# The scores' product with the keys' low parts takes all 128 rows of the query tile, in place of the 64 rows that hold its high parts

## The chip, the cores and the metric

The kernel runs on one core of one Trainium2 chip. The metric is the device time of one execution in microseconds (us). The program is static: each engine works through its own list of instructions in a fixed order, and waits on semaphores where it needs another engine's result.

## What is computed

The reference is a trunk of two layers. Each layer adds half a SwiGLU feed-forward, then a mixer of three head groups with one output projection, then half a second feed-forward. One of the three groups is sparse attention with 8 heads of width 64 in 2 groups. Its selected and its window branch both score every query against the keys of its past; here all 8 blocks of 64 keys are selected, so that both come out as causal attention over the 512 tokens:

```
s = einsum('bqgrd,bgqkd->bgrqk', qb, k_sel) * scale + bias_s      # selected branch
p = masked_softmax(s, d_s >= 0)
o_slc = einsum('bgrqk,bgqkd->bqgrd', p, v_sel)
s = einsum('bqgrd,bkgd->bgrqk', qb, kw) * scale + dense_bias(d_w) # window branch
p = masked_softmax(s, ok_w)
o_win = einsum('bgrqk,bkgd->bqgrd', p, vw)
```

## The kernel before

Nearly all products go through TensorE in a rounded 32-bit format (fp32r), and a 32-bit factor is split in two: a high part that the format holds, and a low part with the rest. A dense product then takes three matmuls in a row into the same PSUM bank (`mm3`, L224 to L226: high by high, high by low, low by high), each with a moving operand of 512 columns.

In the attention a head has only 64 rows of contraction. `nsa_q` (L1052) puts both parts of a query head in one tile of 128 rows: for the even head of a pair (e = 0) the high part is in rows 0 to 63 and the low part in rows 64 to 127, for the odd head (e = 1) the other way round. `nsa_k` (L1035) writes the keys' high part `kh` into both halves of a tile, and the keys' low part `kl` into both halves of another. The matmul at L1156 with `kh` over 128 rows therefore gives (q high + q low) by k high in one go. The matmul at L1159 adds q high by k low; for that it takes only the 64 rows with the high part, rows 0 to 63 for e = 0 and rows 64 to 127 for e = 1.

`scores` (L1143) does one unit: a pair of heads, one block of 128 queries (i = 0 to 3), and the two branches b. For each branch it takes two banks with the tag pS, which has two buffers, and writes four matmuls, of 256, 256, 384 or 512 columns for i = 0 to 3. VectorE then adds the bias and takes the row extreme (L1162), ScalarE exponentiates (L1166), TensorE transposes the weights (`turn`, L1182; its banks have the tags pS and pv by turns) and multiplies them with the values (`mix`, L1198; two heads go side by side, each on 64 columns of the array). There are 16 units in each of the two layers, so 128 matmuls at L1156 and 128 at L1159 in all.

The attention doesn't run alone. Generators for the dense projections, the recurrences, the attention and the output projection are merged by weights (`Weave`), and a scheduler then fixes each engine's order. So the four matmuls of a branch needn't stand together, and dense matmuls, transposes and value products stand between them. The names in the trace: psS is a bank of scores, q, kh and kl the tiles named above, ppt a bank of transposes, pno the attention's output bank, pd a bank of a dense product.

Of the kernel before, what the change touches and what calls it, by code (L numbers as in the profile page):

```python
# [62 lines left out]
class Trunk:  # L63
# [1061 lines left out]
    def nsa(self, st):  # L1125

        nc = self.nc
        v = nc.vector
        V, gates = st["v"], st["g"]
        T, pcT, po = {}, {}, {}  # L1130
        units = [(g, hp, i) for g in range(2) for hp in range(2) for i in range(4)]

        def start(g):
            while "k%d" % g not in st:
                yield 1.0
            T[g] = [self.bias_tile(4 * g + r) for r in range(4)]

        def cmp(g):
            while "vc" not in st:
                yield 1.0  # L1140
            pcT[g] = yield from self.nsa_cmp(g, T[g], st["k%d" % g][1], st["kc"], gates)

        def scores(g, hp, i):  # L1143

            h = 4 * g + 2 * hp
            KS, Q = st["k%d" % g]
            n = 128 * (i + 1)
            nm = max(n, 256)
            qs = slice(i * 128, (i + 1) * 128)
            mx, sm_ = self.s([128, 4], "mx"), self.s([128, 4], "smx")  # L1150
            P = [None] * 4
            for b in range(2):
                kh, kl = KS[b]
                ps = [self.pmt(name="psS", tag="pS") for _ in range(2)]
                for e in range(2):
                    nc.tensor.matmul(ps[e][:, :nm], Q[2 * hp + e][:, qs], kh[:, :nm], start=True, stop=False)  # L1156
                for e in range(2):
                    r = slice(64 * e, 64 * e + 64)
                    nc.tensor.matmul(ps[e][:, :nm], Q[2 * hp + e][r, qs], kl[r, :nm], start=False, stop=True)  # L1159
                for e in range(2):  # L1160
                    p = P[2 * e + b] = self.t2(name="P")
                    v.tensor_tensor_reduce(p[:, :n], T[g][2 * hp + e][:, L - n:], ps[e][:, :n], 1.0, 1e29, OP.add,  # L1162
                                           OP.min, mx[:, 2 * e + b:2 * e + b + 1])
                yield 0.25 + 0.15 * i
            for j in range(4):
                nc.scalar.activation(P[j][:, :n], P[j][:, :n], AF.Exp, bias=mx[:, j:j + 1], scale=-1.0,  # L1166
                                     accum_out=sm_[:, j:j + 1])
            v.tensor_scalar(sm_[:], sm_[:], TINY, None, op0=OP.max)
            v.reciprocal(sm_[:], sm_[:])
            v.tensor_tensor(sm_[:].rearrange("p (e b) -> p e b", e=2), sm_[:].rearrange("p (e b) -> p e b", e=2),  # L1170
                            gates[:, i, 3 * h:3 * h + 6].rearrange("p (e k) -> p e k", e=2)[:, :, 1:3], op=OP.mult)
            for j in range(4):
                v.tensor_scalar(P[j][:, :n], P[j][:, :n], sm_[:, j:j + 1], None, op0=OP.mult)
            return P

        def turn(i, P):
            R = []
            n = 128 * (i + 1)
            for k in range(4):
                pt = self.pmt(name="ppt", tag=("pS", "pv")[k % 2])  # L1180
                for j in range(i + 1):
                    nc.tensor.transpose(pt[:, j * 128:(j + 1) * 128], P[k][:, j * 128:(j + 1) * 128], self.idn[:])  # L1182
                PT = self.t2(name="PT")
                nc.scalar.copy(PT[:, :n], pt[:, :n])
                R.append(PT)
                if k % 2:
                    yield 0.2 * (i + 1)
            return R

        def mix(g, hp, i, R):  # L1190
            if i == 0:
                po[0] = self.pmt(name="pno", tag="po")
            qs = slice(i * 128, (i + 1) * 128)
            for b in range(2):
                for j in range(i + 1):
                    c = slice(g * 128 + 64 * b, g * 128 + 64 * b + 64)
                    for e in range(2):
                        nc.tensor.matmul(po[0][64 * e:64 * e + 64, qs], V[:, j, c], R[2 * e + b][:, j * 128:(j + 1) * 128],  # L1198
                                         start=i == 0 and b == 0, stop=False, skip_group_check=True)
            if i == 3:  # L1200
                nc.tensor.matmul(po[0][:], st["vc"][g][:, hp], pcT[g][:], start=False, stop=True, skip_group_check=True)  # L1201
                self.y[4 + 2 * g + hp] = self.split(po[0][:])
        P, R = {}, {}
        n = len(units)
        lt, lm = self.LAG
        yield from start(0)
        nxt = {}
        for g in range(2):
            nxt[8 * g + self.CMPU] = cmp(g)
        nxt[self.K1] = start(1)  # L1210
        run = []
        for k in range(n + lm):
            if k in nxt:
                run.append((k, nxt[k]))
            for j, q in list(run):
                for _ in range(1 if k < j + 2 else 10 ** 6):
                    try:
                        yield next(q)
                    except StopIteration:
                        run.remove((j, q))  # L1220
                        break
            if k < n:
                P[k] = yield from scores(*units[k])
            if 0 <= k - lt < n:
                R[k - lt] = yield from turn(units[k - lt][2], P.pop(k - lt))
            if 0 <= k - lm < n:
                mix(*units[k - lm], R.pop(k - lm))
                yield 0.44 * (units[k - lm][2] + 1)
# [269 lines left out]
```

## Time and profile before

| | |
|---|---|
| time, median of 3 runs (lowest to highest) | 2116.76 us (2115.8 to 2119.16) |
| the profiled execution: its time, its span | 2116.3 us, 2114.5 us |
| TensorE matmuls busy (share of the span) | 2091.4 us (99%) |
| TensorE weight loads busy | 1695.1 us (80%) |
| VectorE busy | 1188.1 us (56%) |
| ScalarE busy | 786.7 us (37%) |
| GpSimd busy | 82.8 us (4%) |

The span runs from the first to the last instruction in the trace; the profiled execution's time is 1.8 us above its span. An engine's busy time is the union of its instructions' durations. A matmul's duration overlaps the next one's, so what a matmul costs is read from start to start, or from the chain that ended last, which counts from end to end.

### The profile page before, as it was taken

How to read it: one execution, taken by the hardware profiler on the slowest of the kernel's cores; microseconds unless marked ns; L12 is line 12 of the kernel's file. 1: busy time of each engine (PE TensorE's matmuls, PEld its weight loads, DVE VectorE, ACT ScalarE, POOL GpSimd, SP SyncE). 2: the span in 40 equal slices, each digit the busy share in tenths (PEclk: the TensorE clock that was granted, in tenths of full speed). 3: DMA queues.
4: the chain of work that ended last, by engine and by line, in shares of the span. 5: the costliest groups of instructions: out<-in, count | busy, mean ns of one | idle time of the engine just before them, and what ended most of it. 6: DMA issues, size and time to landing. Idle time of an engine off the chain costs nothing.

```text
span 2114.5 us, 28943 instructions
## 1 busy us (share of the span) xinstructions
PE 2091.4 (99%) x11192; PEld 1695.1 (80%) x11192; DVE 1188.1 (56%) x2653; ACT 786.7 (37%) x1455; POOL 82.8 (4%) x153
## 2 busy tenths in 40 slices
PE   8999999999999999999999999999999999999997
PEld 7888888877767888888888888888777678888886
DVE  7864545676765874543544343456777664334435
ACT  5322223445565432232332222243455663222321
POOL 1000000111000100000000000001100000000000
PEclk9999999999999999999999999999999999999999
DMA  5334433433101433432333233234321023333322
GB/s 193 112 104 128 138 127 104 139 113 101 51 16 43 149 117 95 150 97 81 109 100 94 83 114 100 75 115 138 110 75 51 26 80 90 87 93 113 97 82 68
DMA packets 69753, 209.11 MB, mean 99 GB/s; under 512 B 9272, under 2 KB 11912, under 8 KB 69616
## 3 DMA queue, kind: packets, MB, share of 16 engines
q1 hardware_dynamic: 58192, 172.19, 27.1%
q0 software_dynamic: 11280, 35.05, 4.8%
q8 instruction: 88, 1.44, 0.3%
q14 instruction: 49, 0.40, 0.1%
q10 hardware_dynamic: 144, 0.03, 0.0%
HBM read 194.63 MB, written 15.22 MB: 99 GB/s over the span
## 4 chain that ended last, share of the span: by engine, by line
PE 98%; DVE 1%; issue 0%; DMA 0%; ACT 0%; SPq 0%; POOL 0%; DVEq 0%; POOLq 0%
PE pd L224 28%; PE pd L226 27%; PE pd L225 27%; PE pno L1198 2%; PE ppt L1182 2%; PE psS L1159 2%; PE psS L1156 1%; PE plv L875 1%; PE pd L1250 1%; PE pd L1251 1%; PE pd L1252 1%; PE psc L1095 1%; PE pho L945 0%; PE pno L1201 0%; PE pY L784 0%
## 5 line engine op out<-in xcount | busy, mean ns | idle before, releaser
L218 ACT CAST whi<-wraw 128x1024 fp32r<-128x1024 f32 (+5 forms) x377 | 345.4, 917 | 1017.1 <-PE pd L225 703.6
L224 PE MATMUL pd<-xs,whi 128*128 128x512 f32 x1664 | 657.8, 395 | 6.7 <-ACT whi L218 6.1
L226 PE MATMUL pd<-xs,wlo 128*128 128x512 f32 x1664 | 652.2, 392 | 0.0
L225 PE MATMUL pd<-xs,whi 128*128 128x512 f32 x1664 | 650.8, 391 | 0.0
L219 DVE TENSOR_TENSOR wlo<-wraw,whi 128x1024 fp32r<-128x1024 f32 (+5 forms) x377 | 397.0, 1055 | 144.7 <-ACT whi L218 136.1
L224 PEld LDWEIGHTS pd<-xs,whi 128*128 128x128 f32 x1664 | 313.7, 188 | 76.1 <-ACT whi L218 6.1
L226 PEld LDWEIGHTS pd<-xs,wlo 128*128 128x128 f32 x1664 | 313.3, 188 | 66.6 <-issue 0.4
L225 PEld LDWEIGHTS pd<-xs,whi 128*128 128x128 f32 x1664 | 313.6, 188 | 64.1 <-DVE xs L164 1.0
L224 PE MATMUL pd<-hb,whi 128*128 128x512 f32 x682 | 265.8, 390 | 0.0
L226 PE MATMUL pd<-hb,wlo 128*128 128x512 f32 x682 | 265.4, 389 | 0.0
L225 PE MATMUL pd<-hb,whi 128*128 128x512 f32 x682 | 265.4, 389 | 0.0
L293 DVE TENSOR_TENSOR ft<-ft,pd 128x512 f32<-128x512 f32 x88 | 60.5, 687 | 247.5 <-PE pd L226 247.1
L287 DVE TENSOR_TENSOR ft<-pd,rbc 128x512 f32<-128x512 f32 x88 | 60.7, 690 | 189.0 <-PE pd L226 189.0
L226 PEld LDWEIGHTS pd<-hb,wlo 128*128 128x128 f32 x682 | 128.0, 188 | 26.8
L224 PEld LDWEIGHTS pd<-hb,whi 128*128 128x128 f32 x682 | 128.0, 188 | 26.3
L225 PEld LDWEIGHTS pd<-hb,whi 128*128 128x128 f32 x682 | 128.0, 188 | 26.3
L312 DVE TENSOR_TENSOR ft<-pd,r 128x512 f32<-128x512 f32 x62 | 42.9, 692 | 109.3 <-PE pd L226 109.1
L1166 ACT ACTIVATE P<-P,mx 128x128 f32<-128x128 f32 (+3 forms) x128 | 71.7, 561 | 51.9 <-DVE mx L1162 50.5
L1162 DVE CUSTOM_DVE_ANT_0 P<-Tb,psS 128x128 f32<-128x128 f32 (+3 forms) x128 | 60.7, 485 | 49.5 <-PE psS L1159 48.9
L295 DVE TENSOR_TENSOR hb<-ft,hb 128x512 fp32r<-128x512 f32 x88 | 60.3, 685 | 0.0
L288 ACT ACTIVATE ft<-ft 128x512 f32<-128x512 f32 x88 | 55.1, 627 | 13.1 <-DVE ft L287 12.8
L294 ACT CAST hb<-ft 128x512 fp32r<-128x512 f32 x88 | 54.8, 622 | 13.7 <-DVE ft L293 11.8
(388 smaller groups left out, 2158.3 us busy)
## 6 DMA issues: line engine op xcount, KB each, us to landing
wraw<-in_gu SPq DMA_DIRECT2D x175, 512.0 KB, 3.6
wraw<-in_dn SPq DMA_DIRECT2D x64, 384.0 KB, 3.1
wraw<-in_dn SPq DMA_DIRECT2D x64, 320.0 KB, 2.8
wraw<-in_win SPq DMA_DIRECT2D x32, 512.0 KB, 3.5
w<-sp POOLq DMA_DIRECT2D x32, 256.0 KB, 5.8
wraw<-in_wo SPq DMA_DIRECT2D x32, 256.0 KB, 2.6
Tb<-tbl POOLq DMA_DIRECT2D x16, 256.0 KB, 3.6
tbl<-ext POOLq DMA_DIRECT2D x1, 2560.0 KB, 19.7
```

The source lines that it names most:

```text
L218: nc.scalar.copy(h[:, sl], w[:, sl])
L219: self.mark = nc.vector.tensor_tensor(lo[:, sl], w[:, sl], h[:, sl].bitcast(F32), op=OP.subtract)
L224: nc.tensor.matmul(ps, wh, xh, start=first, stop=False)
L225: nc.tensor.matmul(ps, wh, xl, start=False, stop=False)
L226: nc.tensor.matmul(ps, wl, xh, start=False, stop=last)
L287: nc.vector.tensor_tensor(t[:], pg[:], rbc[:], op=OP.mult)
L288: nc.scalar.activation(t[:], t[:], AF.Silu)
L293: nc.vector.tensor_tensor(t2[:], t[:], pu[:], op=OP.mult)
L294: nc.scalar.copy(hb[:, 0, f], t2[:])
L295: nc.vector.tensor_tensor(hb[:, 1, f], t2[:], hb[:, 0, f].bitcast(F32), op=OP.subtract)
L1162: v.tensor_tensor_reduce(p[:, :n], T[g][2 * hp + e][:, L - n:], ps[e][:, :n], 1.0, 1e29, OP.add, OP.min, mx[:, 2 * e + b:2 * e + b + 1])
L1166: nc.scalar.activation(P[j][:, :n], P[j][:, :n], AF.Exp, bias=mx[:, j:j + 1], scale=-1.0, accum_out=sm_[:, j:j + 1])
```

## The change

```diff
                 for e in range(2):
+
                     nc.tensor.matmul(ps[e][:, :nm], Q[2 * hp + e][:, qs], kh[:, :nm], start=True, stop=False)
-                for e in range(2):
-                    r = slice(64 * e, 64 * e + 64)
-                    nc.tensor.matmul(ps[e][:, :nm], Q[2 * hp + e][r, qs], kl[r, :nm], start=False, stop=True)
+                    nc.tensor.matmul(ps[e][:, :nm], Q[2 * hp + e][:, qs], kl[:, :nm], start=False, stop=True)
```

The product with the keys' low part is now over all 128 rows, which adds q low by k low to the sum. It stands directly behind the product with the high part of the same head, into the same bank. No tile, no transfer and no instruction count changes. The program is one line shorter, so that what stands at L1156 and L1159 before is L1157 and L1158 after, and all lines behind are lower by one.

TensorE's order in the first layer, where two pairs of score products of 512 columns stand among value products (pno), dense matmuls (pd) and transposes (ppt). Before:

```order
L1198 MATMUL pno<-PT,vn 64x128 x4
L225 MATMUL pd<-y,whi 128x512
L1156 MATMUL psS<-kh,q 128x512
L1159 MATMUL psS<-kl,q 128x512
L226 MATMUL pd<-y,wlo 128x512
L1156 MATMUL psS<-kh,q 128x512
L1159 MATMUL psS<-kl,q 128x512
L224 MATMUL pd<-y,whi 128x512
L1182 MATMUL ppt<-idn,P 128x128 x2
```
The same place with the change:

```order
L1197 MATMUL pno<-PT,vn 64x128 x4
L1157 MATMUL psS<-kh,q 128x512
L1158 MATMUL psS<-kl,q 128x512
L225 MATMUL pd<-y,whi 128x512
L1157 MATMUL psS<-kh,q 128x512
L1158 MATMUL psS<-kl,q 128x512
L226 MATMUL pd<-y,wlo 128x512
L1181 MATMUL ppt<-idn,P 128x128 x2
L224 MATMUL pd<-y,whi 128x512
```
Each low product still stands behind a high product. The first high product has moved to a place directly behind the value products, and one dense matmul from ahead of it to behind its low product.

TensorE's order a little earlier, where the two heads of a branch stand together. Before:

```order
L1182 MATMUL ppt<-idn,P 128x128 x3
L225 MATMUL pd<-y,whi 128x512
L1156 MATMUL psS<-kh,q 128x256 x2
L1159 MATMUL psS<-kl,q 128x256 x2
L226 MATMUL pd<-y,wlo 128x512
L224 MATMUL pd<-y,whi 128x512
L1182 MATMUL ppt<-idn,P 128x128 x6
```
With the change:

```order
L1181 MATMUL ppt<-idn,P 128x128 x3
L225 MATMUL pd<-y,whi 128x512
L1157 MATMUL psS<-kh,q 128x256
L1158 MATMUL psS<-kl,q 128x256
L1157 MATMUL psS<-kh,q 128x256
L1158 MATMUL psS<-kl,q 128x256
L226 MATMUL pd<-y,wlo 128x512
L1181 MATMUL ppt<-idn,P 128x128 x6
L224 MATMUL pd<-y,whi 128x512
```
The two low products no longer stand side by side; each follows its own high product, which has the same weights.

## Rows read from the trace of the kernel before

**Rows 1.** The page's busy times (part 1) and chain that ended last (part 4).

```profile
PE 2091.4 (99%) x11192; PEld 1695.1 (80%) x11192; DVE 1188.1 (56%) x2653; ACT 786.7 (37%) x1455; POOL 82.8 (4%) x153
...
PE 98%; DVE 1%; issue 0%; DMA 0%; ACT 0%; SPq 0%; POOL 0%; DVEq 0%; POOLq 0%
```
**Rows 2.** Attention stretches: us, busy PE, PEld, DVE, ACT, POOL, PEclk (granted), DMA, GB/s.

```profile
510.00:680.00 170.00, 169.78 (x1078) 120.53 (x1077) 108.60 (x437) 101.21 (x314) 2.15 (x4) 1.00 0.11 35
1553.00:1725.00 172.00, 171.78 (x1088) 122.25 (x1087) 110.55 (x441) 102.75 (x316) 2.15 (x4) 1.00 0.11 35
```
**Rows 3.** Chain that ended last, 595 to 600 us: start us, us, what.

```profile
595.41 0.43 PE pd L225
595.84 0.23 PE psS L1156
596.08 0.42 PE psS L1159
596.50 0.43 PE pd L226
596.93 0.23 PE psS L1156
597.16 0.43 PE psS L1159
597.59 0.43 PE pd L224
...
598.24 0.24 PE pd L225
...
599.86 0.12 PE psS L1156
599.97 0.31 PE psS L1159
```
**Rows 4.** Groups of instructions by form, low products: rows and columns of array, count, mean.

```profile
L1159 PE MATMUL psS<-kl,q 64*128 64x256 f32 x64 | 22.1, 381 | 0.0
...
L1159 PE MATMUL psS<-kl,q 64*128 64x384 f32 x32 | 13.1, 438 | 0.0
...
L1159 PE MATMUL psS<-kl,q 64*128 64x512 f32 x32 | 12.0, 497 | 0.0
```
**Rows 5.** Timeline of TensorE's matmuls, 398 to 401 us: start us, us, instruction.

```profile
398.40 0.28 PE L1250 MATMUL pd<-whi,xs 128*128 128x256 f32 x1
...
400.67 0.28 PE L1251 MATMUL pd<-whi,xs 128*128 128x256 f32 x1
```
**Rows 6.** Timeline of TensorE's matmuls, 575 to 577 us.

```profile
575.37 0.40 PE L1156 MATMUL psS<-kh,q 128*128 128x256 f32 x2
575.69 0.38 PE L1159 MATMUL psS<-kl,q 64*128 64x256 f32 x2
576.00 0.50 PE L226 MATMUL pd<-y,wlo 128*128 128x512 f32 x1
```
**Rows 7.** Timeline of TensorE's weight loads, 568 to 571 us; brackets hold idle time before.

```profile
568.14 0.19 PEld L1156 LDWEIGHTS psS<-kh,q 128*128 128x128 f32 x1
568.57 0.18 PEld L1159 LDWEIGHTS psS<-kl,q 64*128 64x128 f32 x1 [0.24 <-issue]
```
**Rows 8.** Chain's shares by line, 510 to 680 us, then 1553 to 1725 us.

```profile
by line: PE pno L1198 15.0%; PE pd L224 13.7%; PE ppt L1182 13.2%; PE pd L226 12.0%; PE pd L225 11.9%; PE psS L1159 11.6%; PE psS L1156 8.2%; PE psc L1095 3.8%; PE pno L1201 2.5%; PE pch L998 2.2%; PE pho L945 0.9%; PE phb L964 0.9%; PE pct
...
by line: PE pno L1198 14.9%; PE pd L224 13.8%; PE ppt L1182 13.0%; PE pd L226 12.1%; PE pd L225 12.1%; PE psS L1159 11.4%; PE psS L1156 8.1%; PE psc L1095 3.7%; PE pno L1201 2.5%; PE pch L998 2.2%; PE phb L964 1.0%; PE pho L945 0.9%; PE pct
```
**Rows 9.** Waits of TensorE's weight loads, whole span: us in total, times, longest.

```profile
PEld ppt L1182 <- DVE mx L1162: 1.4, 8, 0.2
...
PEld ppt L1182 <- ACT PT L1184: 1.1, 6, 0.2
PEld psS L1156 <- ACT PT L1184: 1.1, 6, 0.2
```
**Rows 10.** Who waited for the score bank psS: us in total, times.

```profile
  DVE P L1162: 48.9, 68
```
## The prediction

> **What bounds the kernel now.** I read the busy times and the chain that ended last first: TensorE's matmuls are busy 99% of the span, and 98% of the chain is TensorE [rows 1]. The change touches TensorE only, and only in the two stretches in which the scores stand, 510 to 680 us and 1553 to 1725 us. There TensorE is busy to within 0.3 us of each stretch, while VectorE is busy 108.6 of 170 us and ScalarE 101.2 [rows 2]. So a microsecond off TensorE's list is a microsecond off the span, as long as the others keep up. The granted clock is 1.00 there [rows 2], the 2.4 GHz level, and as TensorE never rests I don't expect it to move.
>
> Then I read what the low products cost, in the chain, which counts from end to end. Between 595 and 600 us a high product of 512 columns takes 0.23 us, as does a dense matmul between others like it (0.24). The low product behind it takes 0.42 to 0.43, and the dense matmul behind that takes 0.43 as well [rows 3]. With 256 columns the high product takes 0.12 and the low one 0.31 [rows 3]; the pace of full matmuls of 256 columns is the same, 2.27 us over 20 rows in a row, 0.12 a step [rows 5]. The extra is 0.19 to 0.20 us whatever the size, and it falls on each first instruction of a new shape: on the low product, which uses 64 rows of the array against 128 [rows 4], and again on the next instruction with 128. The weight loads show how: the high product's load starts at 568.14 us, ahead of its matmul, but the low product's load waits 0.24 us for nothing that the profile names and starts only at 568.57 [rows 7]. A load for another shape isn't started early; the array finishes first.
>
> The second thing to see is what the 64 rows buy. Where two low products stand side by side, on the two halves of the array, both together take 0.38 us [rows 6], which is what one takes alone (381 ns, [rows 4]). So the second is free there. In TensorE's order before that happens 16 times of a possible 64: the scheduler has split the others.
>
> **The change part by part.** *Shapes.* I counted the order before: 112 low products follow a high product, and pay to enter their shape (the other 16 follow a low product). Behind them, 78 times an instruction of 128 rows and 128 columns comes next and pays to go back; 34 times a value product on 64 columns comes, another shape, which would pay in any case. In the order with the change all 128 low products follow their high product in the same shape, and the 34 value products behind a low product are still 34. The other changes of shape (transposes or dense matmuls to value products and back, and those of the recurrence) are as many as before. So 112 + 78 = 190 changes of shape go. At 0.195 us, the middle of the 0.19 and 0.20 above, that is 37.0 us.
>
> *The lost overlap.* The 16 low products that ran beside another now take their own time: 6 of 256, 2 of 384 and 8 of 512 columns, at 0.12, 0.175 and 0.23 us. The 0.175 is an estimate, midway between its neighbours [rows 3, 5]. That is 0.72 + 0.35 + 1.84 = 2.9 us added.
>
> *Everything else.* Rows of contraction add no columns, and the instruction count stays. The product now reads all of kl, both halves of which were already written and used before, by one head or the other, so it waits for nothing new of weight. The high and low products write the same bank in succession, as the dense matmuls do at full pace [rows 3].
>
> Sum: 37.0 - 2.9 = 34.1 us off.
>
> A second way to the same sum goes by the chain's shares [rows 8]. The low products have 11.6% of 170 and 11.4% of 172 us, 39.3 us together. At full pace the 128 take 64 x 0.12 + 32 x 0.175 + 32 x 0.23 = 20.6 us, so 18.7 go; the 78 instructions behind them give back 0.20 each, 15.6 us. That makes 34.3 us and holds the lost overlap already.
>
> I take 34.1. The profiled execution had 2116.3 us on a span of 2114.5, so I expect 2114.5 - 34.1 + 1.8 = 2082.2 us. The median is 0.46 us above that execution, which makes 2082.7, rounded 2083. The price is bounded by 0.19 and 0.20 (33.2 to 35.1 us). The high products have 8.2% of 170 and 8.1% of 172 us in the chain, 27.9 us [rows 8], against 20.6 at full pace and 28 x 0.20 = 5.6 for entries from value products, so 1.7 us of theirs are waits; if these go too, 36 us are gained.
>
> **A rule that speaks against it.** The row to weigh is that of two low products in 0.38 us [rows 6]. The Trainium skill (TensorE: Matmul & The Clock Gate, the part on packing small matmuls) says that matmuls on different row groups of the array run at the same time, that a matmul of few rows takes as long as one of 128, and that the gain of small shapes is this overlap alone. By that rule only the overlap is counted, and the change can only lose: 2116.8 + 2.9 = 2119.7 us, against 2083 with the price of the shapes. The trace agrees on the overlap and shows, beside it, the price of each change of shape, which is larger.
>
> **The rivals.**
>
> *Time is given back to the softmax.* TensorE's order is fixed, so a shorter TensorE list reaches its waits earlier. TensorE gains some 17 us in each stretch, and VectorE's load rises from 64% to 108.6 of 153 us, 71%. Behind TensorE's matmul waits the whole list. For it: the transposes wait for VectorE's row extremes and ScalarE's copies already, and the scores for a free bank. Against it: these waits are 1.1 to 1.4 us each in the whole span, none above 0.2 us [rows 9], while VectorE waited 48.9 us for scores [rows 10], so it is VectorE that is early. If half the gain goes this way: 2083 + 17 = 2100 us. To bring the change to nothing, each of the 128 score tiles would have to wait 34.1 / 128 = 0.27 us more.
>
> *The shape isn't what costs; slower.* The 0.31 and 0.43 us may belong to the low product itself (its place as last of a group, or its operand kl), not to its shape. Then nothing is freed, and the 16 free ones now cost the full amount: 6 x 0.31 + 2 x 0.37 + 8 x 0.43 = 6.0 us, where 0.37 is again midway. That gives 2122.7 us. If instead pairs are what the 64 rows are for, and all 64 could have been free, the loss would be 64 x 0.161 = 10.3 us against such an order (0.161 is 20.6 / 128), but this order has 16. It decides from the point at which a change of shape costs under 2.9 / 190 = 0.015 us. Against it: the extra is equal for 256 and 512 columns, and it falls on the instruction behind as well [rows 3], which reads no kl.
>
> *It doesn't do what it says.* If the low products' neighbours were of other shapes in any case, only the place of the price would move. That holds for the 34 value products, which are in the sum; were it so for all 78 as well, 112 x 0.195 - 2.9 = 19 us would be left: 2116.8 - 19 = 2098 us.
>
> **How the numbers follow.** The sum as it stands, 2078 to 2088, has a chance of 0.72. Half given back, or half of it never there, 2088 to 2102: 0.17. More than the sum, as waits go with it, under 2078: 0.05. No gain: 0.06, of which slower 0.04. A difference of 0.2%, 4.2 us, is about what a measurement of this kernel can tell. So faster has 0.94, within 0.2% 0.02, slower 0.04. The range is 2076 to 2100: it takes in the 36 us with a little for the runs' own spread, and the half given back.
>
> **What would show it.** Right: the low products appear as 128*128 with 0.12 us (256 columns) and 0.23 (512) in the chain; dense matmuls behind them fall from 0.43 to 0.23; their weight loads start ahead; the low products' 39.3 us in the chain become about 21; TensorE's matmul count stays at 11192. Wrong: low products that stay at 0.31 and 0.43, weight loads that still wait without a named releaser, or new waits of transposes and scores for VectorE and ScalarE that add up to more than some 5 us.

## The result and the profile after

| | before | with the change |
|---|---|---|
| time, median | 2116.86 us (4 runs) | 2091.24 us (4 runs, 2090.71 to 2091.29) |
| ratio, 95% interval | 1 | 0.9877 [0.986, 0.9894] |
| span of the profiled execution | 2114.5 us | 2089.5 us |

The change made the kernel 25.6 us faster; 33.8 us were forecast. The time lies in the range, between the sum and the rival in which half is given back. The kernel before ran beside every set of runs below, at medians of 2116.35 to 2116.86 us, so the sets agree to 0.5 us in it.

The busy times and the chain that ended last (the page's parts 1 and 4) say that TensorE still sets the time; they answer to [rows 1]:

```profile
PE 2064.5 (99%) x11192; PEld 1693.8 (81%) x11192; DVE 1187.2 (57%) x2653; ACT 783.7 (38%) x1455; POOL 82.6 (4%) x153
...
PE 98%; DVE 1%; ACT 0%; DMA 0%; issue 0%; SPq 0%; DVEq 0%; ACTq 0%
```
The chain of the changed kernel, at the place that [rows 3] show of the kernel before (start us, us, what):

```profile
589.43 0.43 PE psS L1157
589.86 0.23 PE psS L1158
590.09 0.24 PE pd L225
590.33 0.23 PE psS L1157
590.56 0.23 PE psS L1158
590.79 0.23 PE pd L226
...
592.95 0.13 PE psS L1157
593.08 0.12 PE psS L1158
```
The low products of 512 columns (L1158) now take 0.23 us in place of 0.42 to 0.43, those of 256 columns 0.12 in place of 0.31, and the dense matmuls behind them 0.24 and 0.23 in place of 0.43. The one piece of 0.43 left is a high product (L1157) directly behind the value products, which enters its shape there. The low product's form and mean duration, from the groups by form, answer to the first of [rows 4]:

```profile
L1158 PE MATMUL psS<-kl,q 128*128 128x256 f32 x64 | 17.5, 281 | 0.0
```
The weight loads of the same pair of products (timeline of PEld: start us, us), which answer to [rows 7]:

```profile
565.21 0.19 PEld L1157 LDWEIGHTS psS<-kh,q 128*128 128x128 f32 x1
565.44 0.19 PEld L1158 LDWEIGHTS psS<-kl,q 128*128 128x128 f32 x1
```
The low product's load starts 0.23 us after the high one's with no wait ahead of it; before, its engine stood idle for 0.24 us. So each step of the price went as forecast. Counted over the matmul records of the two traces, TensorE changes shape 468 times before and 278 times after, 190 fewer, as the order had said. From start to start, the 128 low products took 39.4 us before and 24.0 us after (sums over the records). In the chain their shares are now 6.4% of 158 us and 6.3% of 159 us (510 to 668 and 1541 to 1700 us), 20 us in place of 39.3.

What went against the forecast stands in the waits. The waits of TensorE's weight loads in the first attention stretch of the changed kernel (us in total, times, longest):

```profile
PEld pd L224 <- ACT y L972: 1.6, 1, 1.6
PEld ppt L1181 <- ACT PT L1183: 1.5, 5, 0.6
...
PEld ppt L1181 <- DVE mx L1161: 1.3, 5, 0.3
PEld psS L1157 <- DVE mx L1161: 1.0, 4, 0.3
PEld pd L224 <- DVE x L1362: 0.9, 2, 0.8
...
PEld pno L1197 <- DVE y L973: 0.7, 2, 0.4
```
Rows of the same view for the kernel before:

```profile
PEld ppt L1182 <- DVE mx L1162: 0.7, 4, 0.2
PEld ppt L1182 <- ACT PT L1184: 0.6, 3, 0.2
...
PEld pd L224 <- ACT y L972: 0.2, 1, 0.2
```
Over both stretches, the rows of this view that name a releaser (called the named waits below) add up to 10.0 us before and 20.8 us after. Of these, the waits of scores and transposes for VectorE and ScalarE rose from 6.2 to 9.7 us, and the one for the attention's last output (the row with `ACT y`) from 0.4 to 3.1. The rest of the rise is spread over other places, among them 1.5 us for the value products' bank (`DVE y`).

The first row is a new wait of 1.6 us at the end of the attention; TensorE's matmuls are idle for 0.73 us of it. In the timeline, TensorE has nothing left to do there until ScalarE has copied the last output:

```profile
661.49 1.12 PE L1200 MATMUL pno<-pcT,vc 128*128 128x512 f32 x2
663.34 0.73 PE L224 MATMUL pd<-y,whi 128*128 128x512 f32 x2 [0.73 <-ACT y L972]
664.07 0.50 PE L225 MATMUL pd<-y,whi 128*128 128x512 f32 x1
```
In the kernel before, dense matmuls follow the attention's last products there without a gap:

```profile
673.74 1.13 PE L1201 MATMUL pno<-pcT,vc 128*128 128x512 f32 x2
674.30 0.79 PE L224 MATMUL pd<-y,whi 128*128 128x512 f32 x1
```
The busy times of the two stretches (us, busy PE, PEld, DVE, ACT, POOL, granted clock, DMA share, GB/s) show it as well; in [rows 2] TensorE was busy to within 0.3 us, now 1.4 us are missing in each:

```profile
510.00:672.00 162.00, 160.61 (x1102) 123.83 (x1101) 113.11 (x445) 103.36 (x319) 2.14 (x4) 1.00 0.13 41
1541.00:1702.00 161.00, 159.63 (x1097) 122.99 (x1096) 112.22 (x443) 102.54 (x319) 2.14 (x4) 1.00 0.13 40
```

### The profile page after: what moved, and what is told of

Same layout as the page of the kernel before. It is cut to its first block, busy times and chain, and to the rows that moved or that the text cites. A ratio compares the mean times of both kernels' runs of the same rounds, so it can differ in the third digit from the quotient of the medians.

```text
span 2089.5 us, 28957 instructions
## 1 busy us (share of the span) xinstructions
PE 2064.5 (99%) x11192; PEld 1693.8 (81%) x11192; DVE 1187.2 (57%) x2653; ACT 783.7 (38%) x1455; POOL 82.6 (4%) x153
## 4 chain that ended last, share of the span: by engine, by line
PE 98%; DVE 1%; ACT 0%; DMA 0%; issue 0%; SPq 0%; DVEq 0%; ACTq 0%
PE pd L224 28%; PE pd L226 27%; PE pd L225 27%; PE pno L1197 2%; PE ppt L1181 2%; PE psS L1157 1%; PE plv L875 1%; PE psS L1158 1%; PE pd L1249 1%; PE pd L1250 1%; PE pd L1251 1%; PE psc L1095 1%; PE pho L945 1%; PE pno L1200 0%; PE pY L784 0%; DMA x<-in_x 0%
## 5 line engine op out<-in xcount | busy, mean ns | idle before, releaser
L218 ACT CAST whi<-wraw 128x1024 fp32r<-128x1024 f32 (+5 forms) x377 | 345.2, 917 | 1017.0 <-PE pd L225 711.1
```

What stands on the lines that cost most here:

```text
L218: nc.scalar.copy(h[:, sl], w[:, sl])
```

## The experiments

The change does two things, rows and order, and the first two runs do one each. In all runs the expectation counts 0.195 us for a change of shape.

**The order alone.** From the changed kernel, the low product goes back to 64 rows:

```diff
+                    r = slice(64 * e, 64 * e + 64)
-                    nc.tensor.matmul(ps[e][:, :nm], Q[2 * hp + e][:, qs], kl[:, :nm], start=False, stop=True)
+                    nc.tensor.matmul(ps[e][:, :nm], Q[2 * hp + e][r, qs], kl[r, :nm], start=False, stop=True)
```

> The new order of the four products, but the low product on 64 rows as before. Theory (each change of the array's shape costs TensorE some 0.195 us): all 128 low products now enter their shape, 94 instructions leave it, and none overlaps another: 32 more changes than before (6.2 us) and 2.9 us of overlap lost, so some 2126 us, slower than before. Rival (it is the order, each low product straight behind its high one, that brought the gain): about 2091 us.

Measured: 2129.56 us, ratio 1.0067 [1.0052, 1.0082], slower by 13.2 us. Its chain at the same place:

```profile
597.83 0.43 PE psS L1157
598.26 0.43 PE psS L1159
598.69 0.43 PE pd L225
...
603.53 0.31 PE psS L1157
603.84 0.31 PE psS L1159
```
Every low product (L1159) pays again, 0.43 us here or 0.31, and where another high product follows it (603.53) that pays 0.31 as well. The trace has 500 changes of shape. The order brought none of the gain; on 64 rows it costs.

**The rows alone.** From the kernel before, 128 rows, with both high products ahead of both low ones as they were:

```diff
-                    r = slice(64 * e, 64 * e + 64)
-                    nc.tensor.matmul(ps[e][:, :nm], Q[2 * hp + e][r, qs], kl[r, :nm], start=False, stop=True)
+                    nc.tensor.matmul(ps[e][:, :nm], Q[2 * hp + e][:, qs], kl[:, :nm], start=False, stop=True)
```

> 128 rows for the low product, in the order of before. Theory (the shape costs): the gain of the change, 2088 to 2094 us, with low products of 0.12 and 0.23 us in the chain. Rival (the order brought it): about 2117 us.

Measured: 2086.54 us (2085.2 to 2087.58), ratio 0.9861 [0.9846, 0.9875]. The gain is here, 29.8 us. It lies below the 2088 to 2094 us that were expected, and it is larger than the whole change's by some 4 us: its runs all lie below those of the change (2090.71 to 2091.29), though the 95% intervals of the two ratios overlap a little. With the same kl and the same place as last of its group, the low product of 256 columns takes 0.12 us in the chain:

```profile
592.13 0.14 PE psS L1156
592.28 0.12 PE psS L1158
```
The changes of shape are 278, as in the changed kernel, but the named waits add up to 14.0 us in place of 20.8. The two largest for a score or transpose bank in the first stretch:

```profile
PEld psS L1156 <- DVE mx L1161: 1.1, 5, 0.3
PEld ppt L1181 <- DVE mx L1161: 0.9, 4, 0.3
```
The wait for the attention's last output is back at 0.4 us, as in the kernel before.

**All low products in pairs.** From the kernel before, the low products are tied behind the second high product in TensorE's order (their own two lines stay as they are, one step further in):

```diff
-                    nc.tensor.matmul(ps[e][:, :nm], Q[2 * hp + e][:, qs], kh[:, :nm], start=True, stop=False)
-                for e in range(2):
+                    m = nc.tensor.matmul(ps[e][:, :nm], Q[2 * hp + e][:, qs], kh[:, :nm], start=True, stop=False)
+                with self.tc.issue_after(m.ins):
+                    for e in range(2):
...
```

> 64 rows as before, but TensorE's order is tied so that the two low products of a branch always stand side by side, 64 pairs in place of 16. Theory (shape costs, overlap is worth its own length): 110 changes of shape are paid in place of 190 (15.6 us off) and 48 more low products are free (7.7 us off), so 2094 us if nothing is given back and up to 2106 us if half is, as the first low product now waits for the second high one. Rival (only the overlap counts, shapes cost nothing): 7.7 us off, 2109 us.

Measured: 2106.93 us, ratio 0.9956 [0.9942, 0.997], faster by 9.4 us. All 64 pairs overlap, with starts 3 to 4 ns apart, two low products in the time of one (timeline of TensorE's matmuls):

```profile
599.91 0.50 PE L1156 MATMUL psS<-kh,q 128*128 128x256 f32 x2
600.35 0.38 PE L1160 MATMUL psS<-kl,q 64*128 64x256 f32 x2
```
So the rule of the Trainium skill on packing (TensorE: Matmul & The Clock Gate, the part on packing small matmuls) agrees with the trace in the overlap. The overlap can be had in full, yet the kernel is 15.7 us slower than the changed one. There are 384 changes of shape, and the named waits are the largest of all runs, 26.9 us, mostly for the scores' and the transposes' banks (first stretch):

```profile
PEld ppt L1183 <- DVE mx L1163: 2.1, 8, 0.7
...
PEld psS L1156 <- ACT PT L1185: 1.8, 6, 0.5
PEld psS L1156 <- DVE mx L1163: 1.8, 8, 0.6
PEld ppt L1183 <- ACT PT L1185: 1.5, 4, 1.0
```
The time itself doesn't tell the theory from the rival here, as they lie 3 us apart once half is given back (2106 and 2109 us). The waits do: without a price for the shapes, 7.4 us of overlap gained against 16.9 us of named waits added would leave no gain, and it is 9.4 us.

**Half of the low products.** From the kernel before, 128 rows for the first branch alone:

```diff
-                    r = slice(64 * e, 64 * e + 64)
+                    r = slice(64 * e, 64 * e + 64) if b else slice(0, 128)
```

> 128 rows for the first branch's low products and 64 for the second's, in the order of before: half of the dose. Theory (so much a change of shape, and the later the softmax is met the less is given back): 15 to 18 us off, 2099 to 2102 us. Rival (the gain comes all at once, from the place of one instruction or the end of the attention): about 2091 or about 2117 us.

Measured: 2102.88 us, ratio 0.9937 [0.9923, 0.9952], 13.5 us off, less than the 15 to 18 forecast and 45% of the 29.8 us of the full dose in the same order. The trace has 378 changes of shape, 90 fewer than before, and 12.2 us of named waits. The gain goes by the number of changes (90 of 190 is 47%), not by one place.

**A third bank for the scores.** Of the changed kernel's named waits, 9.7 of 20.8 us are those of scores and transposes, and the bank pT is used once, at the start. From the changed kernel:

```diff
-    PB = {"pd": 2, "pS": 2, "pT": 1, "po": 1, "pv": 2}
+    PB = {"pd": 2, "pS": 3, "po": 1, "pv": 2}
...
-        pre.append(drain(self.dense_x(self.A["gu"][fi, 2, 0], tag="pT")))
+        pre.append(drain(self.dense_x(self.A["gu"][fi, 2, 0], tag="pS")))
```

> The changed kernel with a third bank for the scores and half of the transposes (the bank pT, which lies idle outside the start). TensorE's order comes out with 240 changes of shape in place of 272. Theory (the change's missing 8 us are waits that come up when TensorE's list is shorter, most of them for score and transpose banks): 6.2 us off for the shapes and some 5 off the 20.8 us of named waits, 2080 us. Rival (the waits are for the softmax's results themselves, not for banks, or the missing part lies elsewhere): the shapes alone, 2085 us or more.

Measured: 2077.76 us (2077.39 to 2079.75), ratio to the kernel before 0.9819 [0.9804, 0.9833], 13.5 us under the changed kernel's 2091.24. The named waits fall from 20.8 to 7.3 us, below the kernel before. The largest for these banks in the first stretch are now:

```profile
PEld psS L1157 <- DVE mx L1161: 0.5, 2, 0.3
...
PEld ppt L1181 <- ACT PT L1183: 0.3, 2, 0.2
```
The waits of scores and transposes fall from 9.7 to 3.3 us, near the 5 forecast, which speaks for the banks. The gain is larger than forecast, and with it fell the waits in other places, from 11.1 to 4.0 us (that for the attention's last output from 3.1 to 0.4): the third bank also changed TensorE's order.

**The same bank in the kernel before.** The same edit, made to the kernel before:

> The kernel before with the same third bank: 446 changes of shape in place of 462, and 10 us of named waits of which few are for banks. Theory: 3.1 us off for the shapes and 1 to 2 us of waits, 2112 us, so that the gap to the changed kernel with a third bank comes near the 34 us of the sum. Rival (a third bank helps both alike): 2106 us, the gap stays at 25.

Measured: 2115.72 us, ratio 1.000 [0.9991, 1.001]: no change. That the kernel before got nothing at all wasn't forecast. Its named waits fell from 10.0 to 6.6 us and its changes of shape from 468 to 452, but TensorE's clock was low for longer ahead of the second attention (granted 0.77 from 1500 to 1515 us, 0.89 before) and fell inside it, where the kernel before had 1.00 (columns as in [rows 2]):

```profile
1658.00:1662.00 4.00, 4.00 (x30) 3.15 (x30) 1.16 (x5) 2.03 (x6) 0.00 (x0) 0.60 0.00 0
```
From 1658 to 1662 us the granted clock is 0.60, so a good part of it at the 1.2 GHz level, while TensorE is busy all 4 us. The ten runs go with the clock granted: 2112.80 and 2113.91 us at a mean of 0.996, 2118.09 to 2121.28 at 0.991 to 0.993. At 0.996 the kernel before took 2115.63 to 2117.75 us beside them. So at the same clock the third bank is worth some 3 us here, near the forecast of 2112, and the lower clock of the other runs takes them back in the median. The gap between 64 and 128 rows with a third bank is 38 us by the medians and 35 to 36 at a clock of 0.996, against 25.6 with two banks.

**128 rows, the old order and the third bank.** The edit of the bank, made to the kernel with the rows alone:

> 128 rows in the order of before (the faster of the two orders), with the third bank: 240 changes of shape. Theory: 6.2 us off for the shapes and 2 to 4 us of the 14 us of named waits, 2077 us. Rival (the order no longer matters with a third bank): the same time as the changed kernel with a third bank.

Measured: 2077.51 us (2077.28 to 2078.1), ratio 0.9816 [0.9801, 0.9831]. The time is as forecast, but the rival's point holds as well: with a third bank the order of the four products doesn't matter (2077.51 against 2077.76). This and the run of the changed kernel with a third bank are the fastest versions, 39 us faster than the kernel before and 14 faster than the changed one.

**The end of the attention.** On top of that, the output projection's passes are cut otherwise:

```diff
-    WP = ((0, 1, 2, 3), (4, 5, 6, 7))
+    WP = ((0, 1, 2, 3, 4, 5), (6, 7))
```

> As the run with 128 rows in the order of before and the third bank, but the last pass of the output projection takes 2 of the 8 parts of the mixer's output in place of 4, and the first pass 6. Theory (TensorE waits at the end of the attention for the last parts, and what stands there decides): the first pass starts later and may run past the attention's end; 248 changes of shape cost 1.6 us, the waits for the last parts go or grow by 2 to 3 us, so 2075 to 2081 us. Rival (the end of the attention doesn't matter): 2078.5 us.

Measured: 2101.28 us, ratio 0.9927 [0.991, 0.9943], so 24 us slower than without the edit; the forecast fell. Two stretches of 50 us follow; the attention ends near 663 us in both kernels. The first is of the kernel without the edit, which is also busy for all of 655 to 705 us; the second is of this kernel:

```profile
640.00:690.00 50.00, 50.00 (x299) 40.75 (x298) 36.11 (x100) 30.91 (x54) 3.72 (x7) 1.00 0.38 117
```
```profile
655.00:705.00 50.00, 42.45 (x183) 33.60 (x182) 33.30 (x90) 21.75 (x35) 3.73 (x7) 0.97 0.38 119
```
TensorE is idle for 7.5 of these 50 us in place of none. From 655 to 720 us the weight loads wait 5.2 us for ScalarE's high parts of the next weights (`whi`, L218) and 4.0 us for a row scale from VectorE (`rsy`, L115); behind the second attention, 5.1 and 0.4 us. The short last pass doesn't cover these. The named waits within the attention rose too, from 7.4 to 14.5 us, so together some 22 of the 24 us have a place. That the end matters is shown, but far from the way it was forecast.

## Why the prediction was right, and what was off

The measured 2091.24 us lies outside the 2078 to 2088 that had a chance of 0.72, in the 2088 to 2102 that had 0.17; the range holds it because it took in half the gain lost.

The account of the forecast, so many changes of shape at 0.195 us, the overlap lost, and the named waits gained, can be made for every run against the kernel before. The changes of shape, the free low products and the waits (of the two attention stretches) are counted in each trace; the last column is the difference of the profiled spans.

| run | changes of shape | overlap lost | named waits | sum | measured span |
|---|---|---|---|---|---|
| the change | -190: -37.1 | +2.9 | +10.8 | -23.4 | -25.0 |
| the order alone | +32: +6.2 | +2.9 | +3.6 | +12.7 | +12.1 |
| the rows alone | -190: -37.1 | +2.9 | +4.0 | -30.2 | -31.1 |
| all in pairs | -84: -16.4 | -7.4 | +16.9 | -6.9 | -9.3 |
| half | -90: -17.6 | +2.1 | +2.2 | -13.3 | -13.7 |
| the change, third bank | -222: -43.3 | +2.9 | -2.7 | -43.1 | -38.9 |
| before, third bank | -16: -3.1 | +0.5 | -3.4 | -6.0 | -0.8 |
| rows alone, third bank | -222: -43.3 | +2.9 | -2.6 | -43.0 | -38.2 |
| the same, passes of 6 and 2 | -214: -41.7 | +2.9 | +4.5 | -34.3 | -10.8 |

All values are in us. The sum meets the span within 1 us in three runs and 1.6 in the change itself, and 2.4 in the pairs. With a third bank it promises 4 to 5 us more than came, and in the last run 23 us more. The last run's loss lies mostly behind the stretches in which the waits are counted, as told above. In the kernel before with a third bank, the lower clock is of that size: 0.994 against 0.996 over 2114 us is some 4 us, an estimate from the profiled executions. For the other two the cause stays open.

A named wait isn't lost time by itself. A weight load can wait while a matmul still runs: the kernel before has 10.0 us of such waits, and its matmuls are idle for 0.4 us of both stretches [rows 2]. So a second count was set beside it: the time from each matmul's start to the next one's, less the typical time (median, or mean without outliers, over all runs) for its shape, columns and neighbours' shapes. What is left over rises by 8.7 to 10.3 us with the change, by 2.6 to 4.3 with the rows alone and by some 13.5 in pairs, near the named waits of the table. With a third bank and the old passes it stays within 2.1 us of the kernel before, where the named waits fell by 2.6 to 3.4; that may place a part of the 4 to 5 us.

- **What costs is the change of shape, not the order or the low product itself.** Right: the two runs that split the change put the whole gain on the rows, and half of the rows gave 45% of it. The 190 changes counted also answer the rival in which only the place of the price moves.
- **0.195 us a change, 190 changes.** Right, both: 0.43 to 0.23 us, 0.31 to 0.12, and 190 counted.
- **The lost overlap, 2.9 us.** Right in size as far as the account goes. The run in pairs shows the overlap in full and that it can't pay for its changes of shape.
- **The step that failed** is the part called everything else: it put the order of the four products and all waits at nothing in the sum, and left the waits to a rival. The sum came out 8.5 us too high (34.1 against 25.6), and the named waits rose by 10.8 us. The rows alone show that 4.0 us of it come with a shorter TensorE list in an unchanged order. The rest comes with the new order: the rows alone are 4.7 us faster than the change (2086.54 against 2091.24), mostly by the wait for the attention's last output and those for transposes. I had argued from waits of at most 0.2 us and from VectorE's idle time that VectorE was early. But the waits of scores and transposes fell from 9.7 to 3.3 us once the scores had a third bank, so what counts there is when a bank comes free, and a share of busy time doesn't show that.
- **My sign of trouble** was set at the wrong place. It was new waits of transposes and scores of more than some 5 us; these rose by 3.5 us, and two thirds of the rise came elsewhere.
- **The rival of the time given back** was true to about a quarter in time (8.5 of 34.1 us). By place it was true for the 3.5 us of scores and transposes alone, and it never came near its 0.27 us for each tile.
- **The slower rival** fell with the first two runs: the same low product, last of its group and with the same kl, has its 0.31 and 0.43 us on 64 rows and 0.12 and 0.23 on 128, and on 64 rows the new order costs 13.2 us.

The changed kernel's profile also has something that no term of the sum holds: between 462 and 470 us the granted clock is 0.57, where the kernel before had 0.79 in the same 8 us, ahead of the attention's first score. That score starts 0.8 us later than before (513.4 against 512.6 us). The first row is of the changed kernel, the second of the kernel before:

```profile
462.00:470.00 8.00, 7.71 (x64) 5.62 (x65) 5.99 (x16) 2.94 (x8) 0.00 (x0) 0.57 0.14 53
```
```profile
462.00:470.00 8.00, 7.06 (x69) 5.24 (x69) 7.30 (x17) 3.58 (x10) 0.00 (x0) 0.79 0.24 67
```
Whether the change causes that or the execution, these traces don't tell.

## What to carry to other kernels

A product on a part of the array's rows among full ones paid twice here, 0.19 to 0.20 us when it entered its shape and again when the next full product returned, so padding it to the full shape is worth trying wherever such products stand alone. Price the gain by counting changes of shape in the engine's order, and then look at which banks the shorter list will wait for: here a bank that lay idle was worth another 13.5 us after the change, and some 3 us at the same clock before it. When an edit also moves instructions, run each half by itself: the half that was the point was better alone, by some 4 us with two banks and by nothing with three.

## What the runs showed of the hardware

A change of shape costs about the same, 0.19 to 0.20 us, for 256 and 512 columns and in both directions, and the weight load of the new shape starts together with its matmul (both at 568.57 us before) rather than ahead of it, where the high product's load starts 0.22 us ahead. Two products on the two halves of the array start 3 to 4 ns apart and take the time of one, 0.38 us for 256 columns. I had not expected the clock to fall in a stretch in which the profile shows TensorE busy without a gap: in the kernel before with a third bank, 1658 to 1662 us were granted at 0.60, behind a run of high and low products, transposes and value products that change shape at nearly every step.
